# A diagonal prefix sum: three batches in one PSUM tile of 33 rows, more folding on TensorE, and weighed sums in two tiles

## The chip, the cores and the metric

The kernel runs on one core of a Trainium2 chip. The metric is the device time of one execution in microseconds (us), lower is better.

## The reference

```python
def setup_inputs():
    B, H, W = 4, 4224, 4224
    return {"x": np.random.randn(B, H, W).astype(np.float32)}

def reference(x):
    ps = np.cumsum(np.cumsum(x, axis=1), axis=2)
    diag = np.diagonal(ps, axis1=1, axis2=2)
    return np.cumsum(diag, axis=1).astype(np.float32)
```

The element `diag[i]` is the sum of the square of the first i+1 rows and columns. It grows from one i to the next by a piece of row i and a piece of column i. So the kernel needs, for every i, the sum of row i up to the diagonal and of column i above it, and then two running sums over i. All of x, 285.5 MB of fp32, has to be read once.

## The kernel before

The rows come in strips of 128 partitions x 6 rows, converted to bf16 by the load. Three buffers hold strips. For each strip, VectorE masks the block on the diagonal and sums the rows together with ScalarE; TensorE adds up columns by matmuls with `sel`, a column of ones that selects a row of the PSUM tile `d`. Row g of `d` holds 384 consecutive i.

```python
NBUF = 3
strips = ctx.enter_context(tc.tile_pool(name="strips", bufs=NBUF))
...
for b in range(B):
    r6, r3 = rows6[b % 2], rows3[b % 2]
    d = psum_d.tile([NG, GW], FP32, name="d")        # 11 x 384, two buffers
    ...
            mu = mup.tile([P, f, f * P], BF16, name=f"mu{f}")
            block = strip[:, :, r0:hi]
            nc.vector.tensor_mul(out=mu, in0=block, in1=um)
            nc.vector.tensor_sub(out=block, in0=block, in1=mu)
            for q in range(f):
                for h in range(nw):
                    columns(g + h, 0, GW, mu[:, q, h * GW : (h + 1) * GW])
                if ws > wp:
                    act_sum(acc[:, q, 0:1], strip[:, q, wp:ws])
            row_sums(acc[:, :, 1], strip[:, :, ws:hi])
    ...
```

Each batch ends with its own closing: row sums go into `d`, then one sum per row of `d`, carries between the rows by two small matmuls, two scans, and an output.

```python
        pu = smalls.tile([NG, 2], FP32, name="pu")
        c12 = smalls.tile([NG, 2, GW], FP32, name="c12")
        row_sums(pu[:, 0:1], d)
        masked(c12[:, 1, :], d, to_end, pu[:, 1:2])
        ...
        matmul(carry_ps, earlier, pu, start=True)
        matmul(carry_ps[:, 1:2], apart, pu[:, 0:1])
        carry = smalls.tile([NG, 2], FP32, name="carry")
        nc.vector.tensor_copy(out=carry, in_=carry_ps)
        for i, src in enumerate((d, c12[:, 0, :])):
            nc.vector.tensor_tensor_scan(out=c12[:, i, :], data0=ones_row,
                data1=src, initial=carry[:, i : i + 1], op0=ALU.mult, op1=ALU.add)
```

The last 384 rows of the last batch come in another order, so that little work is left when the last byte lands: the head (their columns at the diagonal) at the very start, then, as the last transfers of all, part a (256 rows, two pieces) and part b (128 rows, five pieces). Part a is shared out: TensorE folds some columns with an identity matmul into 512 columns of PSUM, ScalarE and VectorE sum the others. Part b is summed by ScalarE and VectorE; VectorE's instruction for it, `pair`, adds two halves of its columns and sums the result. What comes of parts a and b is weighed by small matmuls into one PSUM tile `fin`, to which VectorE adds what the scans give for these rows; `yl` and `ye` are the sums that go out last:

```python
        c0, c1 = acuts[1]
        cp = c0 + 768
        fold_in(fold_a, part_a, c0, cp, 256)
        for h in range(2):
            act_sum(asum[:, h, 3:4], part_a[:, h, cp:c1])
        row_sums(asum[:, :, 4], fold_a)
        ...
        fin = psum_s.tile([1, GW], FP32, name="fin")
        ...
        weigh(arows[:, 0:1], weights, 0)
        weigh(arows[:, 1:2], weights, P)
        ...                       # sums of part b into bsum
        finish(0, M0)             # VectorE reads fin[:, 0:256]
        for k in range(2):
            for i in (1, 0):
                weigh(bsum[:, k, i : i + 1], weights4, M0 + (k + 1) * R)
        ...
        finish(M0, GW)            # VectorE reads fin[:, 256:384]
```

## Time and profile before

| | before |
|---|---|
| time, median of the first 3 runs | 667.39 us (667.06 to 668.84) |
| span of the profiled execution | 665.7 us |
| read from memory | 285.47 MB, 429 GB/s over the span |
| busy: VectorE, TensorE, ScalarE | 50%, 31%, 21% of the span |
| mean granted TensorE clock | 0.661 |

The page gives the share of time that each engine is busy, in 40 slices as tenths, and the same for the 16 DMA engines. Busy shares do not say what sets the time: the chain of waits on this page puts nearly half on VectorE.

```profile
DVE 47%; another core or an unknown queue 45%; DMA 5%; PE 2%; issue 1%; DVEq 0%; POOLq 0%
...
strip<-in_x_dram POOLq DMA_DIRECT2D x19, 6336.0 KB, 76.7
```

The first line is the chain by engine. The second is from the DMA issues (count, KB written each, median us from issue to landing): a strip is asked for 76.7 us before it has landed, though its transfer takes 30 us. The chain passes through VectorE because VectorE released the buffer, long before the transfer could begin.

In the timeline of TensorE at the end (start, duration, instruction, idle before it):

```profile
662.37 0.71 PE L208 MATMUL fin<-weights,bsum 128*1 128x96 f32 x8 [0.76 <-DVE yl L474]
662.92 0.50 PE L208 MATMUL fin_e<-weights,esum 128*1 128x32 f32 x6
```

TensorE idles 0.76 us until VectorE has read the first 256 columns of `fin`, although the matmuls that wait write other columns of it.

### The profile page before, as it was taken

The numbers are of one execution on the slowest core, as the hardware profiler recorded it, in microseconds if no ns is written. First come the engines' busy times: TensorE is split into PE (matmuls) and PEld (weight loads), VectorE is DVE, ScalarE is ACT, GpSimd is POOL, SyncE is SP. The second block draws the span as 40 slices with busy tenths as digits, with TensorE's granted clock in tenths as the row PEclk, the third lists the DMA queues.
The fourth block names the chain that finished last, engine by engine and source line by source line (L and its number), as shares of the span: only waits on it lengthen the run. The fifth ranks groups of instructions, "written<-read, shape, count | busy, mean of one in ns | idle before, by whom it ended". The sixth has DMA issues, their size and how long they took to land.

```text
span 665.7 us, 2562 instructions
## 1 busy us (share of the span) xinstructions
PE 204.5 (31%) x981; PEld 97.8 (15%) x981; DVE 334.6 (50%) x165; ACT 140.3 (21%) x226; POOL 31.3 (5%) x59
## 2 busy tenths in 40 slices
PE   0081522403117143130221623504032263250427
PEld 0030211101003021110110311202011031120203
DVE  3161625456916153454782524436288343352767
ACT  0001120406300103040630020304063002030436
POOL 7000000000000000000000000000000000001000
PEclk9995857656558585675755957666565586766758
DMA  9999999999999999999999999999999999999998
GB/s 203 219 219 219 219 218 218 219 212 207 220 221 216 219 219 215 219 215 216 212 219 222 218 215 219 216 216 218 216 213 219 221 213 220 216 216 218 218 207 162
DMA packets 7670, 143.23 MB, mean 215 GB/s; under 512 B 702, under 2 KB 1002, under 8 KB 2154
## 3 DMA queue, kind: packets, MB, share of 16 engines
q0 software_dynamic: 7296, 142.47, 99.9%
q1 hardware_dynamic: 362, 0.61, 0.3%
q8 instruction: 7, 0.11, 0.1%
q14 instruction: 5, 0.04, 0.0%
HBM read 285.47 MB, written 0.07 MB: 429 GB/s over the span
## 4 chain that ended last, share of the span: by engine, by line
DVE 47%; another core or an unknown queue 45%; DMA 5%; PE 2%; issue 1%; DVEq 0%; POOLq 0%
DVE acc L230 29%; DVE mu L320 8%; DVE strip L321 8%; DMA strip<-in_x_dram 5%; PE d L208 1%; DVE c L436 1%; PE fold L208 1%; DVE pu L230 0%; DVE c L250 0%; DVE rows L360 0%; DVE acc L335 0%; PE carry_ps L208 0%; DVE pair L239 0%; PE fin L208 0%
## 5 line engine op out<-in xcount | busy, mean ns | idle before, releaser
L208 PE MATMUL d<-strip,sel 128*11 128x384 bf16 x603 | 138.7, 403 | 377.7 <-DMA strip<-in_x_dram 377.7
L225 ACT ACTIVATE dump<-strip 128x416 bf16<-128x416 bf16 (+8 forms) x112 | 128.4, 1146 | 522.0 <-DMA strip<-in_x_dram 519.3
L320 DVE TENSOR_TENSOR mu<-strip,um 128x4608 bf16<-128x4608 bf16 (+1 forms) x24 | 52.4, 2183 | 307.1 <-DMA strip<-in_x_dram 307.0
L230 DVE TENSOR_REDUCE acc<-strip 128x6 f32<-128x4608 bf16 (+6 forms) x23 | 196.0, 8523 | 0.8
L208 PEld LDWEIGHTS <-sel 128*11 128x11 bf16 x849 | 86.2, 102 | 522.3 <-issue 479.3
L208 PE MATMUL d<-mu,sel 128*11 128x384 bf16 x243 | 49.1, 355 | 45.8 <-DVE mu L320 45.8
L321 DVE TENSOR_TENSOR strip<-strip,mu 128x4608 bf16<-128x4608 bf16 (+1 forms) x24 | 52.4, 2183 | 1.0
L76 POOL DMA_DIRECT2D strip<-in_x_dram x24 | 16.4, 686 | 543.0 <-DVE acc L230 281.7
L225 ACT ACTIVATION_READ_ACCUMULATOR dump<-strip 128x1 f32 x112 | 20.9, 186 | 0.0
L208 PE MATMUL d<-ident,rows 128*11 128x128 f32 x24 | 5.2, 379 | 16.8 <-DVE rows L369 16.8
L208 PE MATMUL fold<-strip,ident_h 128*128 128x480 bf16 x8 | 3.4, 598 | 10.7 <-DMA strip<-in_x_dram 10.7
L208 PE MATMUL d<-halves,rows 128*11 128x64 f32 x48 | 5.5, 296 | 0.0
L94 DVE MEMSET um<- 128x4608 bf16 (+1 forms) x2 | 4.9, 2458 | 1.1 <-issue 1.1
L208 PEld LDWEIGHTS d<-ident,rows 128*11 128x11 f32 x24 | 2.6, 119 | 18.5 <-DVE rows L369 11.7
L95 POOL TENSOR_SCALAR_AFFINE_SELECT um<-um 128x4608 bf16<-128x4608 bf16 (+1 forms) x2 | 5.2, 2611 | 2.4 <-DVE um L94 2.4
L208 PEld LDWEIGHTS d<-halves,rows 128*11 128x11 f32 x48 | 5.1, 134 | 1.5 <-issue 1.5
L230 DVE TENSOR_REDUCE pu<-d 11x1 f32<-11x384 f32 x4 | 2.2, 546 | 5.2 <-PE d L208 5.2
L436 DVE TENSOR_TENSOR_SCAN c<-ones_row,carry,c 11x384 f32<-11x384 f32 x4 | 4.0, 1005 | 0.1
L436 DVE TENSOR_TENSOR_SCAN c<-ones_row,carry,d 11x384 f32<-11x384 f32 x4 | 4.0, 1000 | 0.1
L409 POOL DMA_DIRECT2D strip<-in_x_dram x5 | 2.7, 557 | 26.4 <-DMA strip<-in_x_dram 26.4
L208 PEld LDWEIGHTS <-ident_h 128*128 128x128 bf16 x14 | 1.6, 119 | 13.8 <-issue 13.5
L230 DVE TENSOR_REDUCE parts<-strip 128x3 f32<-128x3072 bf16 x1 | 3.4, 3353 | 0.0
(87 smaller groups left out, 37.2 us busy)
## 6 DMA issues: line engine op xcount, KB each, us to landing
strip<-in_x_dram POOLq DMA_DIRECT2D x19, 6336.0 KB, 76.7
strip<-in_x_dram POOLq DMA_DIRECT2D x5, 3168.0 KB, 59.9
strip<-in_x_dram POOLq DMA_DIRECT2D x1, 1080.0 KB, 49.9
strip<-in_x_dram POOLq DMA_DIRECT2D x1, 768.0 KB, 52.9
strip<-in_x_dram POOLq DMA_DIRECT2D x3, 256.0 KB, 54.1
head<-in_x_dram SPq DMA_DIRECT2D x1, 528.0 KB, 4.0
strip<-in_x_dram POOLq DMA_DIRECT2D x1, 192.0 KB, 43.2
strip<-in_x_dram POOLq DMA_DIRECT2D x1, 64.0 KB, 28.6
```

The costliest lines, as they stand in the source:

```text
L76: nc.gpsimd.dma_start(out=o, in_=x[b, r0 : r0 + f * P, :].rearrange("(p f) w -> p f w", f=f))
L94: nc.vector.memset(um, 1.0)
L95: nc.gpsimd.affine_select(out=um, in_=um, compare_op=ALU.is_gt, fill=0.0, base=0, pattern=[[-1, f], [1, f * P]], channel_multiplier=-f,)
L208: nc.tensor.matmul(o, lhsT=lhsT, rhs=rhs, start=start, stop=False, skip_group_check=True)
L225: nc.scalar.activation(out=dump[:, :w], in_=src, func=ACT.Copy, accum_out=acc)
L230: nc.vector.reduce_sum(out=acc, in_=src, axis=AX.X)
L320: nc.vector.tensor_mul(out=mu, in0=block, in1=um)
L321: nc.vector.tensor_sub(out=block, in0=block, in1=mu)
L409: nc.gpsimd.dma_start(out=part_b[:, sb, c0:c1], in_=x[b, r0 : r0 + R, :TB].rearrange("r (k c) -> r k c", k=4)[:, :, c0:c1],)
L436: nc.vector.tensor_tensor_scan(out=c12[:, i, :], data0=ones_row, data1=src, initial=carry[:, i : i + 1], op0=ALU.mult, op1=ALU.add,)
```

## The change

The intent: one closing in place of three for the first three batches; less work for ScalarE at the end, by folding nearly all of part a on TensorE; no waiting between TensorE and VectorE on the weighed sums; and no separate load of the last 128 x 128 diagonal block, which now comes with the head.

```diff
-        tc.tile_pool(name="psum_d", bufs=2, space=bass.MemoryType.PSUM)
+        tc.tile_pool(name="psum_d", bufs=1, space=bass.MemoryType.PSUM)
-    HC = 528
-    head = last.tile([P, 2, HC], FP32, name="head")
+    HC = GW
+    head = last.tile([P, F, HC], FP32, name="head")
 ...
-        r6, r3 = rows6[b % 2], rows3[b % 2]
-        d = psum_d.tile([NG, GW], FP32, name="d")
+        r6, r3 = rows6[b // LB], rows3[b // LB]
+        if b in (0, LB):
+            rows = NG if b else NW                 # 11 or 33
+            d = psum_d.tile([rows, GW], FP32, name=f"d{rows}")
 ...
-            if not whole and s == 0:
-                diag_b = last.tile([P, P], BF16, name="diag_b")
-                nc.gpsimd.dma_start(out=diag_b, in_=x[b, TB:N, TB:N])
 ...
-        sum_up(a6)                                  # add, then copy
-            nc.vector.tensor_copy(out=r6[...], in_=a6[ps, :, :, 1])
+            sum_up(r6[ps, k : k + 2 * ns : 2, :], a6[ps])
 ...
+        if b < LB - 1:
+            continue                                # no closing for batches 0 and 1
 ...
-            cp, ca = c0 + 768, c0 + 768 + 1152
-            fold_in(fold_a, part_a, c0, cp, 256, start=True)
+            cp, ca = c0 + 1792, c0 + 1792 + 256
+            fold_in(fold_a, part_a, c0, c0 + 1280, 256, start=True)
 ...
+        if not whole:
+            fold_in(fold_a, part_a, c0 + 1280, cp, 256)
 ...
-        cp = c0 + 768
-        fold_in(fold_a, part_a, c0, cp, 256)
-        for h in range(2):
-            act_sum(asum[:, h, 3:4], part_a[:, h, cp:c1])
+        fold_in(fold_a, part_a, *acuts[1], 256)
 ...
-        fin = psum_s.tile([1, GW], FP32, name="fin")
+        fin_a = psum_s.tile([1, M0], FP32, name="fin_a")
+        fin_b = psum_s.tile([1, P], FP32, name="fin_b")
 ...
-        for k, ca in ((0, 512), (1, 448)):
+        for k, ca in ((0, 480), (1, 416)):
```

Cut: the masks between groups for 33 rows, constants that share a tile, and the renamed helpers.

## The prediction

> **What bounds the kernel now.** I read the slices of the page first, then its DMA part, then the busy times by stretch between the strips' landings, and last the timeline of the final 10 us, VectorE first, then TensorE.
>
> The slices and the DMA part of the page:
>
> ```profile
> DVE  3161625456916153454782524436288343352767
> DMA  9999999999999999999999999999999999999998
> GB/s 203 219 219 219 219 218 218 219 212 207 220 221 216 219 219 215 219 215 216 212 219 222 218 215 219 216 216 218 216 213 219 221 213 220 216 216 218 218 207 162
> ...
> q0 software_dynamic: 7296, 142.47, 99.9%
> ...
> HBM read 285.47 MB, written 0.07 MB: 429 GB/s over the span
> ```
>
> The reader is to see that the DMA engines are at 9 tenths or more in 39 of 40 slices, while VectorE is on average half idle (50% of the span), ScalarE and TensorE more. The GB/s row counts the bf16 bytes that are written; the fp32 bytes that are read are twice that.
>
> Busy time by stretch, each cut from one strip's landing to the next's (columns: stretch, its length, PE, PEld, DVE, ACT, POOL busy, granted clock, DMA share, GB/s):
>
> ```profile
> 1.33:34.82 33.49, 0.00 (x0) 0.00 (x0) 9.15 (x22) 0.77 (x1) 12.19 (x26) 1.00 1.02 222
> ...
> 170.00:199.99 29.99, 4.07 (x25) 2.54 (x25) 15.86 (x17) 6.24 (x6) 1.43 (x2) 0.50 1.01 218
> 199.99:229.92 29.93, 12.86 (x67) 6.40 (x67) 10.06 (x3) 0.01 (x1) 0.71 (x1) 0.73 1.01 217
> ...
> 529.10:559.24 30.14, 13.84 (x67) 6.66 (x67) 10.07 (x4) 0.00 (x0) 0.71 (x1) 0.67 1.00 216
> 559.24:589.17 29.93, 10.96 (x58) 5.43 (x58) 12.83 (x7) 3.86 (x13) 1.10 (x2) 0.67 1.01 217
> ```
>
> A strip of six rows per partition (12.98 MB read) lands every 29.9 to 30.0 us, whether VectorE is busy 10 or 16 us of it. The strip that lands at 199.99 took 29.99 us although the first batch's closing work and its scans (184.7 to 188.3 us) ran in that stretch; the next, with no scan in it, took 29.93. So nothing that computes holds the transfers back. The chain of waits gives VectorE 47% and "another core or an unknown queue" 45%: it follows the buffer release backwards and isn't a list of what limits; each strip's VectorE work (10 to 19 us) is over long before the next lands.
>
> The end is the only place where computation is exposed. Timeline of VectorE there (start, duration, instruction, idle before it):
>
> ```profile
> 657.42 1.00 DVE L436 TENSOR_TENSOR_SCAN c<-ones_row,carry,d 11x384 f32<-11x384 f32 x1
> 658.46 1.00 DVE L436 TENSOR_TENSOR_SCAN c<-ones_row,carry,c 11x384 f32<-11x384 f32 x1
> 659.39 0.65 DVE L230 TENSOR_REDUCE asum<-fold_a 128x2 f32<-128x512 f32 x1
> ...
> 661.52 0.46 DVE L239 SCALAR_TENSOR_TENSOR pair<-strip 128x288 f32<-128x288 bf16 x1 [0.85 <-DMA strip<-in_x_dram]
> ...
> 661.90 0.41 DVE L474 TENSOR_TENSOR yl<-fin,c 1x256 f32<-1x256 f32 x1
> 662.46 0.39 DVE L239 SCALAR_TENSOR_TENSOR pair<-strip 128x224 f32<-128x224 bf16 x1 [0.15 <-DMA strip<-in_x_dram]
> ...
> 662.78 0.29 DVE L239 SCALAR_TENSOR_TENSOR pair<-strip 128x128 f32<-128x128 bf16 x1
> ...
> 663.12 0.28 DVE L474 TENSOR_TENSOR yl<-fin,c 1x128 f32<-1x128 f32 x1
> 663.50 0.18 DVE L512 TENSOR_TENSOR ye<-fin_e,yl 1x32 f32<-1x32 f32 x1
> ```
>
> VectorE waits for data at 661.52 (0.85 us idle) and at 662.46 (0.15 us). Whatever is done before 661.5 is therefore hidden, up to that 0.85 us. From the last landing (about 662.7) there are 0.8 us of reduction and combination to 663.50, 0.2 us to the last output transfer at 663.71, and 2.0 us of that transfer to the end at 665.7. The measured time of the profiled run was 667.42, so 1.7 us lie outside the span.
>
> **What the Trainium skill says.** (1) "DMA: Bandwidth & Descriptors", section "Anatomy of one DMA — SWDGE (gpsimd) path": one transfer costs about 2.0 us plus bytes over 436 GB/s. The trace agrees: the first strip with the 0.54 MB of the head beside it would be an estimated 2.0 + 13.52/0.436 = 33.0 us, and it took 33.5; steadily it is 12.98 MB in 29.95 us, 433 GB/s. The same page's "Specifications" put an HBM limit of some 358 GB/s per core; here, with one core running, 429 GB/s were measured over the whole span, and the measurement decides. The kernel is thus at the page's fabric ceiling of 435 GB/s. (2) The same "Specifications" name 512 B as the least transfer at line rate. The diagonal block that the change drops is 128 pieces of 512 B read and 256 B written. (3) "TensorE: Matmul & The Clock Gate", section "Part 1: The HAM clock gate": TensorE runs at half clock after idling and at full clock after some 3.4 us of activity. The trace fits: 0.50 granted at 633.9 to 654.1 us, 0.94 and 1.00 behind it, when eight folds and the closing matmuls follow one another. (4) "PSUM — Partial Sum Buffer", section "PSUM bank collisions raise a hardware error": an engine's access must be guarded by bank. This is why TensorE's weighed sums waited 0.76 us for VectorE's read of the first 256 columns in the kernel before, and why two tiles take that wait away.
>
> **The change part by part.**
>
> One scan for three batches. Removed at the ends of the first two batches: 0.55 + 0.53 + 0.07 + 0.15 + 1.00 + 1.00 = 3.3 us of VectorE each, nine matmuls on the row sums, four matmuls of carries, and two of three small outputs. TensorE passes the same 384 columns per matmul into 33 rows rather than 11, and a weight load of 33 columns lies between the 0.10 us of 11 and 0.12 of 128. The work that goes lies in stretches where VectorE then idles 11.6 us (188.4 to 199.99): on the path 0 us. Copies of the row sums folded into the additions (0.18 us each) and the memsets that go (0.2 us) are hidden too: 0 us.
>
> The setup. Halves are added on GpSimd, masks and ones share tiles, the head has three row blocks and is summed in a slightly longer VectorE stretch at 17 to 20 us. The first strip lands at 34.8 us, and GpSimd's next transfer is not due before the first buffer is free at 45 us: 0 us.
>
> Bytes. Before, head 128 x 2 x 528, part a 128 x 2 x 3696, part b 128 x 4096, diagonal 128 x 128 elements; after, 128 x 3 x 384, 128 x 2 x 3840, 128 x 3840. Both add up to 3 x 128 x 4224, so the fp32 bytes read are identical. What goes is one transfer of small pieces: the stretch that holds it is 30.14 us against 29.91 (mean of the two behind it). Its 65.5 kB take 0.15 us at 433 GB/s and come back in the others, so some 0.08 us is gained. The head writes 49 kB more in fp32, with pieces of 1536 B rather than 2112 B; I set no more than 0.05 us against it. Net: -0.05 us.
>
> The tail up to 661.5. Part a grows by 144 columns, so its two pieces land 0.34 us later (147 kB over 433 GB/s), at 654.4 and 658.1; the part-b pieces shrink from 1.21 to 1.13 us each, and the last of them lands where it did, near 662.7. TensorE now folds six matmuls of 512 columns behind 658.1, at the 0.27 us of the three in the trace (0.81 us): 1.6 us, to 659.7, where VectorE, out of its scans at about 659.5, takes 0.65 us for the fold, then 0.16 and the first pair at 660.8 to 661.2. VectorE is 0.5 us later than before but still idles some 0.3 us until the third part-b piece lands near 661.5. ScalarE sheds 2 x 1.16 + 2 x 0.84 us and adds 2 x 0.4. All hidden: 0 us.
>
> From the last landing. The last piece stays 256 columns (a pair of 128, 0.29 us). The pair ahead of it is 208 wide rather than 224: 16 columns at 0.96 ns per column, the slope between 288 (0.46) and 128 (0.29) being nearer 1.06, make -0.02 us. The two tiles for the weighed sums take away TensorE's 0.76 us wait, but the closing sum waits for VectorE's last pair, not for that; I give it -0.05 us. The closing 2.0 us of output stay.
>
> Sum: 0 + 0 - 0.05 + 0 - 0.02 - 0.05 = -0.12 us. From 667.39 this is 667.27; I predict 667.2.
>
> **The rivals.** First, the added folds overrun the slack. For it: VectorE's margin falls from 0.85 to an estimated 0.3 us, and at half clock six folds take twice 1.6 us; the reduction then starts 1.6 us later, of which the margin of 0.3 and the 0.15 us at 662.46 swallow 0.45, so that the end moves by up to 1.15 us, to 668.4. Against it: the clock was 1.00 there, and TensorE gets more work just ahead of it. Second, the scans had delayed buffers, and with their removal the transfers speed up: 3.3 us twice would make 661. Against it: the stretches with scans are no longer than those without (29.99 against 29.93 us), and the transfers are queued 77 us before they land. Third, the tail wait on the weighed sums was on the path, and its 0.76 us are saved: 666.6. Against it: VectorE runs from 662.46 to 663.40 without a gap, whatever TensorE does.
>
> **Range and chances.** The three runs before span 667.06 to 668.84, far more than the change; the transfers alone decide. 8 in 10: 666.3 to 668.3. Two per cent is 13 us, some four times everything that the tail holds exposed (3.0 us), so faster 0.01, slower 0.01, same 0.98.
>
> **What would show it.** Right: DMA row unchanged at 9; strips every 29.9 us; the stretch with the diagonal 0.1 to 0.2 us shorter; VectorE still idle before the second or third pair; last landing near 662.6; 3.0 us from it to the end. Wrong: a gap between transfers, a strip rate other than 433 GB/s, or no idle time on VectorE before the closing pairs, with TensorE's clock at 0.5 behind 654 us.

## The result, and the profile after

The changed kernel took 667.9 us (median of 6 runs, 667.14 to 669.62), the kernel before 667.77 us in 6 runs. A ratio here is the mean time of one kernel's fast runs over that of the other's of the same rounds, so not quite the ratio of the medians: 1.0005, with a 95% interval of 0.9987 to 1.0023. Measured again on the same chip as some of the experiments, it was 0.9995 (0.9976 to 1.0014). The two kernels are equal within what these runs can tell; the differences of a few tenths below are read from single traces, and spans are given to 0.1 us.

From the page of the changed kernel, slices and DMA part:

```profile
DVE  3261625456906153454780524436388243352767
DMA  9999999999999999999999999999999999999998
GB/s 206 219 219 219 219 219 215 212 210 218 219 218 219 219 220 218 218 213 212 216 218 218 217 219 219 218 219 211 215 216 219 219 214 220 216 219 216 214 208 162
...
HBM read 285.47 MB, written 0.07 MB: 429 GB/s over the span
```

The row of the DMA engines is unchanged, as are the bytes read and their rate. VectorE lost 8.2 us of busy time (334.6 to 326.4), and nothing came of it.

Busy time by stretch between landings (columns as before: stretch, length, PE, PEld, DVE, ACT, POOL busy, clock, DMA share, GB/s):

```profile
170.00:200.12 30.12, 1.17 (x4) 0.45 (x4) 12.58 (x8) 6.25 (x6) 1.43 (x2) 0.50 1.00 215
529.11:559.06 29.95, 13.77 (x67) 6.75 (x67) 10.07 (x4) 0.00 (x0) 0.71 (x1) 0.67 1.01 217
559.06:588.95 29.89, 10.83 (x58) 5.51 (x58) 12.26 (x3) 3.87 (x13) 1.10 (x2) 0.67 1.01 217
```

The first is the stretch that held the first batch's closing. VectorE's work in it fell from 15.86 to 12.58 us, and it took no less time (30.12 against 29.99 us). The second no longer holds the diagonal block and is 0.19 us shorter than before (29.95 against 30.14).

The end of the changed kernel, VectorE and then TensorE:

```profile
659.42 0.69 DVE L246 TENSOR_REDUCE asum<-fold_a 128x2 f32<-128x512 f32 x1
...
661.41 0.44 DVE L255 SCALAR_TENSOR_TENSOR pair<-strip 128x272 f32<-128x272 bf16 x1 [0.68 <-DMA strip<-in_x_dram]
...
662.33 0.38 DVE L255 SCALAR_TENSOR_TENSOR pair<-strip 128x208 f32<-128x208 bf16 x1
...
662.66 0.29 DVE L255 SCALAR_TENSOR_TENSOR pair<-strip 128x128 f32<-128x128 bf16 x1
...
662.87 0.27 DVE L480 TENSOR_TENSOR yl<-fin_b,c 1x128 f32<-1x128 f32 x1
663.29 0.18 DVE L521 TENSOR_TENSOR ye<-fin_e,yl 1x32 f32<-1x32 f32 x1
```

```profile
657.93 1.46 PE L226 MATMUL fold_a<-strip,ident_h 128*128 128x512 bf16 x6 [0.35 <-DMA strip<-in_x_dram]
...
661.77 0.72 PE L226 MATMUL fin_b<-weights,bsum 128*1 128x96 f32 x8
662.77 0.49 PE L226 MATMUL fin_e<-weights,esum 128*1 128x32 f32 x6 [0.28 <-DVE pair L255]
```

VectorE still waits for data at 661.41, now 0.68 us rather than 0.85. The six folds took 1.46 us and delayed nothing that counts. TensorE's sums of part b start at 661.77, without the wait for `yl`, and the last `yl` follows 0.21 us after the start of VectorE's last pair, where it was 0.34 before.

### The profile page after: what moved, and what is told of

Read it like the earlier page. It is cut to its first block, busy times and chain, and to the rows that moved or that the text cites. A ratio compares the mean times of both kernels' runs of the same rounds, so it can differ in the third digit from the quotient of the medians.

```text
span 665.4 us, 2461 instructions
## 1 busy us (share of the span) xinstructions
PE 201.7 (30%) x948; PEld 103.7 (16%) x948; DVE 326.4 (49%) x136; ACT 136.9 (21%) x222; POOL 31.8 (5%) x62
## 4 chain that ended last, share of the span: by engine, by line
another core or an unknown queue 44%; DVE 42%; DMA 11%; issue 1%; POOL 0%; PE 0%; DVEq 0%; POOLq 0%
DVE acc L246 27%; DMA strip<-in_x_dram 11%; DVE mu L333 7%; DVE strip L334 7%; DVE c L440 0%; POOL strip L411 0%; DVE rows L348 0%; PE d L226 0%; POOL strip L400 0%; DVE pu L246 0%; PE fin_e L226 0%; DVE c L266 0%; DVE pair L255 0%; PE carry_ps L226 0%
## 5 line engine op out<-in xcount | busy, mean ns | idle before, releaser
L226 PE MATMUL d<-strip,sel 128*33 128x384 bf16 (+1 forms) x603 | 140.7, 408 | 397.9 <-DMA strip<-in_x_dram 397.9
L241 ACT ACTIVATE dump<-strip 128x416 bf16<-128x416 bf16 (+6 forms) x110 | 125.1, 1138 | 520.5 <-DMA strip<-in_x_dram 517.8
L226 PEld LDWEIGHTS <-sel 128*33 128x33 bf16 (+1 forms) x849 | 94.9, 112 | 534.1 <-issue 495.9
L226 PE MATMUL d<-mu,sel 128*33 128x384 bf16 (+1 forms) x243 | 48.9, 353 | 45.4 <-DVE mu L333 45.4
L96 DVE MEMSET um<- 128x6144 bf16 x1 | 5.2, 5178 | 1.2 <-issue 1.2
L226 PE MATMUL d<-ones_all,rows 128*33 128x128 f32 (+1 forms) x12 | 2.3, 347 | 5.4 <-DVE rows L348 5.4
L226 PE MATMUL fold_a<-strip,ident_h 128*128 128x512 bf16 x13 | 3.3, 380 | 0.3 <-DMA strip<-in_x_dram 0.3
L226 PEld LDWEIGHTS d<-halves,rows 128*33 128x33 f32 (+1 forms) x24 | 2.5, 150 | 0.7 <-issue 0.5
L226 PE MATMUL d<-halves,rows 128*33 128x64 f32 (+1 forms) x24 | 2.6, 284 | 0.0
L348 DVE TENSOR_TENSOR rows<-acc 64x30 f32<-64x30 f32 (+2 forms) x12 | 2.1, 177 | 0.9
```

The source lines that it names most:

```text
L96: nc.vector.memset(um_all, 1.0)
L226: nc.tensor.matmul(o, lhsT=lhsT, rhs=rhs, start=start, stop=False, skip_group_check=True)
L241: nc.scalar.activation(out=dump[:, :w], in_=src, func=ACT.Copy, accum_out=acc)
L348: nc.vector.tensor_add(out=o, in0=acc[..., 0], in1=acc[..., 1])
```

## The experiments

Eleven kernels were run. All but the pair with reused strips are correct. A number in brackets after a time is its range. The kernel before ran beside them on the same chips, between 667.08 and 670.64 us.

**The changed kernel again.** No edit.

> The changed kernel once more, unaltered, with more rounds than the first measurement. Theory (transfers set the time, and what the change moves lies beside them): ratio to the kernel before 0.9995 to 1.0005, that is 0.1 to 0.3 us less than it at most, inside the noise. Rival (removed scans speed up the transfers): 0.99. Rival (added folds overrun the tail): 1.001 to 1.002, with the last landing to the end longer than the 2.9 to 3.0 us of before.

667.77 us (667.36 to 668.86), ratio 0.9995 (0.9976 to 1.0014). The interval contains no gain of 1%, so the removed scans did not speed up the transfers. From the third part-b piece, where VectorE waits for data, to the end its trace takes 4.04 us; the first trace of the changed kernel has 3.99, the kernel before 4.18.

**One tile for the weighed sums.**

```diff
-        fin_a = psum_s.tile([1, M0], FP32, name="fin_a")
-        fin_b = psum_s.tile([1, P], FP32, name="fin_b")
+        fin = psum_s.tile([1, GW], FP32, name="fin")
+        fin_a, fin_b = fin[:, :M0], fin[:, M0:]
```

(The second start flag goes too, as both parts are one tile now.)

> The changed kernel with the two PSUM tiles of the weighed sums put back into one. Theory: TensorE's sums of part b wait again for VectorE's read of the first 256 columns; from the start of the second-last pair to the end the trace takes 3.24 us as in the kernel before, against 3.07 in the changed one (0.15 us more). Rival (the prediction's step: VectorE's own order sets this end): 3.07 us stay. Total time within noise in both cases.

667.8 us (667.49 to 668.99), ratio 0.9999 (0.9981 to 1.0017): nothing in the total, as both theories said. The trace tells them apart:

```profile
661.78 0.44 DVE L255 SCALAR_TENSOR_TENSOR pair<-strip 128x272 f32<-128x272 bf16 x1 [0.73 <-DMA strip<-in_x_dram]
...
662.65 0.38 DVE L255 SCALAR_TENSOR_TENSOR pair<-strip 128x208 f32<-128x208 bf16 x1
...
662.76 0.71 PE L226 MATMUL fin<-weights,bsum 128*1 128x96 f32 x8 [0.50 <-DVE yl L480]
...
663.51 0.28 DVE L480 TENSOR_TENSOR yl<-fin,c 1x128 f32<-1x128 f32 x1 [0.18 <-PE fin L226]
```

VectorE's last `yl` now waits for TensorE (0.18 us idle), which had waited 0.50 us for VectorE's read of the first 256 columns. From 662.65 to the end at 666.0 are 3.35 us; the changed kernel has 3.07 and 3.13 in its two traces. From the third part-b piece it is 4.22 us against 3.99 to 4.04. So the two tiles are worth 0.2 to 0.3 us in this tail. That is more than the change as a whole gained there. The traces show the chain (ends of matmuls are modelled): TensorE's weighed sums of part a end 0.47 us after the start of the pair on the third part-b piece (662.25 against 661.78), in the kernel before 0.09 us after it (661.61 against 661.52). In one tile VectorE's first read waits for these sums, and the sums of part b wait for that read. With two tiles the sums of part a end 0.52 us after the start of this pair, with less folding (below) 0.24, so the folds make most of the lateness; the new order of the sums was not run by itself.

**More folds.** Twelve folds ahead of the last six, into a spare tile.

```diff
+        junk_ps = psum_s.tile([P, 2, 256], FP32, name="fold")
+        for k in range(2):
+            fold_in(junk_ps, part_a, *acuts[1], 256, start=k == 0)
         fold_in(fold_a, part_a, *acuts[1], 256)
```

> The changed kernel with twelve more folds (twice the six of part a's second piece) ahead of the last six, into a spare PSUM tile; the result stays right. Theory: 12 folds at 0.24 us are 2.9 us on TensorE; VectorE's idle 0.68 us before the second pair swallows part, so from the landing of the last piece to the end 2.2 to 2.6 us more, span 667.6 to 668.1 if the transfers run as before. Rival (there is more slack in the tail): under 1 us more. Rival (TensorE falls to half clock there): more than 4 us.

670.64 us (669.84 to 671.16), ratio 1.0036 (1.0018 to 1.0053), span 668.6 us.

```profile
658.93 2.75 PE L226 MATMUL fold<-strip,ident_h 128*128 128x512 bf16 x12 [0.55 <-DMA strip<-in_x_dram]
...
663.02 0.69 DVE L246 TENSOR_REDUCE asum<-fold_a 128x2 f32<-128x512 f32 x1 [2.91 <-PE fold_a L226]
```

From the first fold of the second piece to the end there are 9.67 us; in the changed kernel 7.47 and 7.52. That is 2.2 us more for 2.6 us of folds (661.52 to 658.93): the idle 0.68 us swallowed some 0.4. The span is 0.5 us above the 667.6 to 668.1 expected: in this trace the transfers ran about 1 us later (last strip of six rows at 619.88 us, 618.88 in the changed kernel). TensorE did not fall to half clock: it was granted 1.00 from 658.9 to 663.0 us, and twelve folds took 2.75 us. So the tail can be overrun, and the change stays short of it.

**Less folding.** Part a shared out as in the kernel before, in the changed kernel.

```diff
-            cp, ca = c0 + 1792, c0 + 1792 + 256
+            cp, ca = c0 + 768, c0 + 768 + 1152
 ...
-        fold_in(fold_a, part_a, *acuts[1], 256)
+        fold_in(fold_a, part_a, 0, 768, 256)
+        for h in range(2):
+            act_sum(asum[:, h, 4:5], part_a[:, h, 768:1536])
```

> The changed kernel with part a shared out among the engines as in the kernel before: three folds by TensorE for each of its two pieces, ScalarE 1152 and 768 columns of each row block, VectorE the rest (640 columns of the first piece, as this is now 144 longer). Theory (all of this ends before the third part-b piece lands): from the start of TensorE's fold of the second piece to the end 7.5 us as in the changed kernel, total within noise. Rival (the folds moved to TensorE pay): 0.3 us or more longer, ScalarE late with its part-b sums.

(The 640 columns in this text are a slip: VectorE's rest is 384 columns of each row block.) 668.33 us (667.11 to 669.88), ratio 0.9991 (0.9974 to 1.0009). From the fold of the second piece (658.31) to the end (665.8) there are 7.49 us, as in the changed kernel.

```profile
661.79 0.44 DVE L255 SCALAR_TENSOR_TENSOR pair<-strip 128x272 f32<-128x272 bf16 x1 [0.78 <-DMA strip<-in_x_dram]
```

VectorE idles 0.78 us before the third part-b piece here, 0.68 with the folds. Who sums part a makes no difference to the end: ScalarE was not late before the change, so relieving it gains nothing.

**More work for VectorE at the ends of the first three batches, in three doses.**

```diff
             sum_up(r3[:, row_of(LG), :], acc3[:, 0])
+            for k in range(n):                     # 4, 9 or 14
+                filler = smalls.tile([P, 1], FP32, name="filler")
+                row_sums(filler, um_all)           # 128 x 6144 bf16, 6.4 us
```

Four:

> The changed kernel with four reductions over 6144 bf16 columns (6.4 us each, 25.6 us) added on VectorE at the end of each of the first three batches: nearly five times the work on VectorE that the shared scan removed per batch, 76.8 us in all. Theory (buffers are released far ahead of need): no change, ratio 0.999 to 1.001. Rival (work at the batch ends delays the buffers and with them transfers): 667.9 + 3 x (25.6 - 17.2 idle) = 693 us.

667.6 us (667.32 to 668.95), ratio 0.9996 (0.9978 to 1.0014).

Nine:

> The filler with nine reductions, 57.6 us on VectorE at each of the first three batch ends (172.8 us in all). Theory (a buffer is wanted two strips, some 60 us, after its own strip landed): the first strip of the next batch is started at about 241 us and its buffer free at 251, before 260 when it is wanted, so no change: ratio 0.998 to 1.004. Rival (the slack is the idle time seen on VectorE there, 17 us plus one strip's 20 us): some 20 us more per batch, 728 us.

667.66 us (667.19 to 668.93), ratio 0.9988 (0.9966 to 1.001).

Fourteen:

> The same filler with fourteen reductions, 89.6 us at each of the first three batch ends. Theory (three buffers let VectorE fall behind by some 60 us before transfers starve): from 183 us the filler runs to 273, the first strip of the next batch is released near 283 instead of 210, whereas its buffer is wanted at 260: some 24 us exposed per batch, 72 in all, 740 us (range 715 to 760). If the slack were as small as the idle time seen on VectorE (17 us): 3 x 72 = 217 us more, 885.

755.82 us (754.36 to 756.28), ratio 1.1307 (1.1282 to 1.1331).

VectorE's timeline with nine: the first three strips of the second batch and the fourth.

```profile
240.90 2.55 DVE L333 TENSOR_TENSOR mu<-strip,um 128x4608 bf16<-128x4608 bf16 x1
250.94 2.55 DVE L333 TENSOR_TENSOR mu<-strip,um 128x4608 bf16<-128x4608 bf16 x1
263.19 2.55 DVE L333 TENSOR_TENSOR mu<-strip,um 128x4608 bf16<-128x4608 bf16 x1
289.96 2.56 DVE L333 TENSOR_TENSOR mu<-strip,um 128x4608 bf16<-128x4608 bf16 x1 [12.44 <-DMA strip<-in_x_dram]
```

VectorE takes up the strip that is due at 200 us only at 240.90, and the fourth strip still lands at 289.96, as in the kernel before (289.84). With fourteen, the busy time by stretch shows where it breaks:

```profile
273.55:283.59 10.04, 7.44 (x29) 3.73 (x29) 9.97 (x5) 0.00 (x0) 0.00 (x0) 0.59 0.00 0
283.59:318.13 34.54, 14.75 (x82) 8.28 (x80) 26.44 (x7) 0.01 (x1) 1.99 (x3) 0.77 0.96 201
```

Until the first strip's buffer is free at 283.59 us the DMA share is 0.00, and the fourth strip lands at 318.13, 28.1 us later than in the changed kernel. The fourth strips of the third and the last batch land 55.4 and 88.0 us later (509.82 against 454.38, 706.83 against 618.88): the three delays make up the whole 88 us. The estimate was 24 us per batch: it counted from 260 us and left out that a load into an empty queue took 34.5 us from release to landing rather than 29.9. So 172.8 us of added VectorE work cost nothing, and the slack at a batch's end lies between 58 and 90 us. The closing of a batch that the change removed (5.3 us) is far inside it.

**Strips used again, so that the transfers do not set the pace.** In both kernels the first three strips serve all of the first three batches, and no further strip is loaded for these.

```diff
-            strip = prefetched.pop(0) if prefetched else None
-            if strip is None:
+            if whole:
+                strip = prefetched[s % NBUF]
+            else:
 ...
-        strip = strip_tile()
+        strip = prefetched[2] if whole else strip_tile()
         if whole:
-            load_rows(strip[:, :F], b, T0)
```

The kernel before:

> The kernel before, with the three strips of the first loads used again for all of the first three batches (wrong results on purpose), so that VectorE and not the transfers sets the pace for these. Estimate from the trace: 35 us to the first landing, 3 x 85.8 us of VectorE (80.5 for strips, 5.3 from the last reduction to the second scan), last batch loads from 32 us before the end of that at 433 GB/s for 165 us, 3 us tail: about 430 us.

474.74 us (472.79 to 475.39). The estimate missed by 45 us: it let VectorE run through the first batch from 35 us on, but the three strips land 30 us apart, so that the first batch ended at 160 us and not at 121. That is 39 of the 45.

The changed kernel:

> The changed kernel with the same reuse of three strips (wrong results on purpose). Theory (the shared scan's gain is real on VectorE and only hidden by the transfers): two closings of 5.3 us less, and some 0.4 us of row copies in each of three batches: 10 to 12 us less than the kernel before with reuse, about 419 us, 2.5 per cent. Rival (the shared scan saves nothing even where VectorE sets the pace): equal to it.

460.64 us (460.38 to 462.36): 14.1 us or 3.0% less than the kernel before with the same edit, by the medians. The same change that gave nothing gives 3% where VectorE sets the pace. VectorE's timeline at the first strips of the second and of the third batch, the kernel before and then the changed one, both with reuse:

```profile
160.32 2.54 DVE L320 TENSOR_TENSOR mu<-strip,um 128x4608 bf16<-128x4608 bf16 x1
...
246.62 2.54 DVE L320 TENSOR_TENSOR mu<-strip,um 128x4608 bf16<-128x4608 bf16 x1
```

```profile
154.18 2.55 DVE L333 TENSOR_TENSOR mu<-strip,um 128x4608 bf16<-128x4608 bf16 x1
...
234.62 2.55 DVE L333 TENSOR_TENSOR mu<-strip,um 128x4608 bf16<-128x4608 bf16 x1
```

The second batch took 86.30 us before and 80.44 after, 5.86 less. The first batch, counted from the third landing, gained 5.71. Together 11.6 us, within the 10 to 12 expected. Of the rest (the spans differ by 14.4 us), 1.7 us lie in the third batch (in the kernel before VectorE waited 1.34 us for TensorE there), 0.8 us in the last batch and 0.4 us in the landing of the third strip.

**48 extra small loads.** Three behind each later strip of six rows, 65.5 kB each, once as 128 pieces of 512 B and once as 16 of 4096 B.

```diff
                 load_rows(strip, b, s * F2 * P)
+                for k in range(3):
+                    extra = last.tile([P, P], BF16, name=f"extra{k}")
+                    nc.gpsimd.dma_start(out=extra, in_=x[LB, TB:N, TB:N])
```

> The changed kernel with three extra loads of a 128 x 128 block (pieces of 512 B) behind each later strip of six rows, 48 in all, 3.15 MB. Theory as predicted: 0.15 us for its bytes and 0.08 us for its small pieces, 0.23 us each, 11 us in all, 679 us. If small pieces cost nothing beyond their bytes: 7.3 us, 675. Strips with three extras land 0.45 to 0.7 us later than the 29.9 us of the others.

678.17 us (678.06 to 678.36). With the large pieces, which go as fp32 into the head's tile:

> Control to the 48 extra loads in small pieces: the same 65.5 kB each, read as 16 rows of 4096 B (and written as fp32 into a tile no longer needed). Theory (0.15 us for the bytes, the rest for small pieces): strips with three extras land 0.45 us later than 29.88, not 0.61, and the whole takes 7.3 us more than the changed kernel, 675 us. Rival (the bytes or the number of transfers alone make it): 678 us as with small pieces.

677.74 us (676.83 to 678.48). The strips of the third batch land 30.49 us apart with small pieces (369.18 to 491.14 us, four strips) and 30.38 with large ones (368.78 to 490.30), against 29.9 without. Per extra load that is 0.20 and 0.16 us, where the bytes alone make 0.15 at 433 GB/s. In the total it is 0.21 and 0.18 us, each give or take 0.03, by the ratios to the kernel before on the same chip (1.0149 and 1.0132; the two ran on different chips), so the totals do not tell small from large. By the strips' spacing the small pieces cost some 0.04 us of a load, half of the 0.08 predicted. The theory for the control held for the spacing (0.49 us later per three extras, 0.45 expected) and not for the total (678 us and not 675). The control is not perfect: it writes fp32, twice the bytes, into 16 partitions. In both runs GpSimd waits for earlier extras before it issues more, so that strips are asked for 59 us before they land rather than 77; the DMA row stays at 9.

## Why the prediction was right

The time on record was 667.2 us, and 667.9 was measured, inside the range. By the steps:

- *What bounds the kernel.* Right. The transfers set the time: the DMA row did not change, and neither 172.8 us of added VectorE work nor another sharing out of part a moved the total. Two details: one strip of the kernel before, the third, came 30.46 us after the one before it, outside the 29.9 to 30.0 named; and that the rate of reading is near the fabric ceiling that the prediction cites does not show which part of the path limits it, as only half of these bytes, some 217 GB/s by the GB/s row, are written into the strips.
- *One scan for three batches: 0 us.* Right, and shown from both sides. With the transfers in place it gave nothing; with the strips reused it gave 5.7 and 5.9 us per batch. The instructions counted in the prediction make 3.3 us of these, the waits around them and the copies the rest. The rival "the scans had delayed buffers" is refuted by the doses.
- *Setup: 0 us.* Agrees, though VectorE's stretch on the head came at 20.3 to 22.8 us, not at 17 to 20; the first landing is 34.64 us against 34.82, less than the spread of first landings told below.
- *Bytes: -0.05 us.* The stretch with the diagonal block got 0.19 us shorter, as named. The 0.08 us for its small pieces were mis-sized: by the strips' spacing these cost some 0.04. Too small to matter in the total.
- *Tail up to 661.5: 0 us.* Right, with one term mis-sized: VectorE's margin shrank to 0.68 us, not 0.3. The second piece came at 657.93 rather than 658.1, six folds took 1.46 us to their end rather than 1.6, so the reduction started at 659.42 rather than 659.7; and the prediction put the first pair at 660.8, where its own terms (659.7 + 0.65 + 0.16) give 660.5. The rival of overrun folds is real at twelve folds more (2.2 us), not at six.
- *From the last landing: -0.07 us.* The sum came out near, the terms did not, and that they made up for each other is luck. From the start of the second-last pair to `ye` it is 1.04 us before and 0.96 in both traces of the changed kernel, 0.08 less. The narrower pair gave none of it: from its start to the last pair's there are 0.32 us before and 0.33 after. The step that failed is "the closing sum waits for VectorE's last pair, not for that", and with it "without a gap, whatever TensorE does". In the kernel before, the last `yl` starts at 663.12, just as TensorE's sums of part b end (662.37 + 0.71 = 663.08), 0.34 us after the start of the last pair; without the wait it is 0.21. So the two tiles bring `yl` forward by 0.13 us, not 0.05, of which 0.04 is lost again before `ye`, which now follows the end of TensorE's `fin_e` (662.77 + 0.49 = 663.26, `ye` at 663.29). With the tile put back the tail was 0.2 to 0.3 us longer. The rival that gave this wait its full 0.76 us was wrong too. That the wait comes of the bank rule that the prediction cites is not shown: the runs show that it comes and goes with the shared tile.

What stays open: the runs of one kernel differ by up to 3.3 us (the kernel before from 667.34 to 670.64 on one chip), and the traces taken, all of short runs, do not show what the longer ones spend it on. Differences below about 1 us were therefore never visible in the total: it confirms that nothing of that size happened, and the 0.12 us of the sum are seen in single traces alone.

## What to carry to other kernels

Before removing work, measure the slack of the buffer chain by adding work: three doses of filler told more than any busy share, and the dose that finally hurt, 89.6 us, was some fifteen times the 5.8 us that the change removed per batch. Where transfers run at their ceiling throughout, only what lies behind the last landing can be gained, and there one asks which of two engines the closing instruction really waits for; VectorE showed no idle time before its last sum, and yet TensorE's chain held it back by 0.13 us. To see whether an optimisation is real but hidden, run it where its engine sets the pace.

## What the Trainium skill lacked or had wrong

- "DMA: Bandwidth & Descriptors", section "Bandwidth": the sentence by which the HBM side (some 358 GB/s) binds transfers from HBM lacks its condition. It holds, as the same section says beside its measured table, with both cores of a pair streaming. Here, with one core running, 429 GB/s over the whole span and 433 GB/s from strip to strip were measured. The prediction took the 358 for a limit of one core by itself, which the section, read as a whole, does not say.
- The same page has a fixed cost per transfer and an overhead for small descriptors; it does not say what is left of them in a queue that is already full. Here 65.5 kB behind a strip took 0.20 us in pieces of 512 B, written as 256 B, and 0.16 us in pieces of 4096 B, where the bytes alone make 0.15.
- No page that I read has the spread at the start of a full queue: with the loads issued at the same 1.33 us, the first strip landed between 34.64 and 36.62 us in thirteen traces, and the third between 95.24 and 96.48.
